# A decoder layer in which gated linear attention runs beside the branch projections and its inputs are computed in pairs

## The chip, the cores and the metric

The kernel runs on one core of a Trainium2 chip. TensorE multiplies matrices (PE in the profile; PEld are its weight loads, which overlap the products), VectorE (DVE) does elementwise arithmetic, ScalarE (ACT) activations, copies and biases, GpSimd (POOL) fills and a few transfers, and SyncE (SP) issues most of the transfers. The metric is device time of one execution in microseconds, lower is better; a kernel's time is the median of several executions.

## What is computed

One layer of a decoder for 512 prompt positions and 8 x 8 sample positions, 576 columns in all, model width 2048, float32. One projection of the input feeds three token mixers: S5 (a diagonal state space model), GLA (gated linear attention, 4 heads) and a convolution over 31 taps. Each mixer's output is multiplied by its gate path, projected to the model width, scaled by a sigmoid merge gate and summed; the sum goes through w_o.

```python
proj = x @ w_in + b_in
(s5_u, s5_z, q, k, v, a_low, gla_z, ca, cb, cz, gates) = jnp.split(proj, _split_points(), axis=-1)
y_s5, s5_re_new, s5_im_new = s5_mixer(s5_u, ...)
y_s5 = jax.nn.gelu(y_s5)
y_s5 = y_s5 * jax.nn.sigmoid(y_s5 @ w_glu + b_glu)
br_s5 = (y_s5 * jax.nn.silu(s5_z)) @ p_s5
o_gla, gla_new = gla_mixer(q, k, v, a_low, gla_s, gla_w_a2, gla_b_a, gla_norm_g)
br_gla = (o_gla * jax.nn.silu(gla_z)) @ p_gla
y_c, conv_new = conv_mixer(ca, cb, conv_buf, conv_w, conv_b, conv_ln_g, conv_ln_b)
br_conv = (y_c * jax.nn.silu(cz)) @ p_conv
g_s5, g_gla, g_conv = jnp.split(jax.nn.sigmoid(gates), N_BRANCH, axis=-1)
out = (g_s5 * br_s5 + g_gla * br_gla + g_conv * br_conv) @ w_o
h = DN_ALPHA * x + out
h = h + jax.nn.sigmoid(h @ w_pg) * (p @ w_pe)
return layer_norm(h, ln_g, ln_b), ...
```

Inside conv_mixer, g = ca * sigmoid(cb) is convolved per channel with 31 taps, then normalised over the channels.

## The kernel before, in words

**Precision and products.** A float32 operand is split into a high part in the type fp32r (`hi`, an ACT copy) and the rest (`lo`, a DVE subtraction). A product of two operands is three matmuls: hi by hi, hi by lo, lo by hi. Columns are held as two halves of 288, so that a matmul has the form 128x288 with a contraction of 128.

**Jobs.** The big products are a list of jobs of three kinds, which `run_jobs` works off in order. A *single* makes one tile of 128 output rows. With 16 contraction tiles it is 96 matmuls (line 433); with 8, in w_glu and the three branch projections p_gla, p_s5 and p_conv, it is 48 ("short"). A *pair* makes two tiles of 128 rows at once by seven half sized products in the manner of Strassen and Winograd (`PRODUCTS`, line 462): 7 x 24 = 168 matmuls where two singles need 192. It needs sums of the weights (DVE, `raw<-raw` and `raw<-raw,sl`) and sums of the input, the forms S1 to S4, which `make_forms` prepares once for w_in and `m_forms` once more for w_o. After some of the seven products ACT or DVE copies or adds a partial result out of PSUM: "a" after the first (from `mm`) and the second (from `aux`). A *quad* (line 543) is a small product for w_pe.

**Background work.** Everything else (S5's scan, GLA's decay and heads, the convolution, its norm, the splitting of the mixers' outputs) is written as generators that are advanced by `pump` between pieces of the jobs: BG_RATE 1.1 in full singles, BG_SHORT 0.5 in short ones, BG_PAIR 0.2 in pairs, each times the length of the piece; a generator's `yield` names the cost of the step it has done. Groups in SLOW are a lane of their own. `need(key)` drives the background until a result is there. A scheduler then orders the instructions of each engine; tiles come from 71 slots of 128x576 floats in SBUF, and a generator waits when too few are free.

**The order of the work.** First 8 jobs for s5_u with the S5 blocks beside them, 6 gate tiles as singles, the job `a` (the decay's low rank input), then the 16 tiles k, q and v of the four heads as singles, head after head (`plain` keeps them in SBUF), with a GLA head spawned after each head's tiles; after that 4 more gate tiles as singles and `make_forms`. Then the pairs: 8 for the convolution's inputs ca and cb, 12 for s5_z, gla_z and cz, 19 for the other 38 gate tiles; the convolution tiles run beside them. A convolution tile is, per tap, one DVE operation on 512 prompt columns and one on the 64 sample columns (line 98). Then w_glu (8 short jobs), p_gla, p_s5 and p_conv (16 each), whose results are multiplied by their gates and summed in SBUF in `self.A` by `br_job`; beside p_conv `m_forms` makes the forms of the sum for w_o, a quad follows, then w_o in 8 pairs, another quad, w_pg and the layer norm.

Of the kernel before, what the change touches and what calls it, by code (L numbers as in the profile page):

```python
# [30 lines left out]
BG_RATE, BG_SHORT, BG_PAIR = 1.1, 0.5, 0.2  # L31
WIDTH = dict(s5=3)
SLOW = ("forms", "conv", "conv_norm")
# [5 lines left out]
NFILL = (0, 0, 0, 4, 6)  # L39
# [4 lines left out]
class K:  # L44
# [274 lines left out]
    def run_jobs(self):  # L319
# [201 lines left out]
        for u in range(first, nu):  # L521
            ji, k0, n = units[u]
            if self.jobs[ji][0] == "pair" or self.jobs[ji][1].shape[0] < D:
                self.reserve = 0
            while npr < nu and (npr <= u + 1 or at[npr] - at[u] < PREP):
                prep(npr)
                npr += 1
            load_to(u)
            if n is None:
                run_pair(u)  # L530
                continue
            kind, w, col, xs, evac, before, after, dual = self.jobs[ji]
            if kind == "quad":
                if before is not None:
                    before()
                xh, xl = xs()
                hv = halves.pop(u)
                for j in range(4):
                    ps = self.ps_mm.tile([128, 1024], F32, name="mm")
                    for k, (_, _, hi, lo) in enumerate(hv):  # L540
                        for lh, rh, a, b in ((hi, xh, k == 0, False), (hi, xl, False, False), (lo, xh, False, k == 1)):
                            for o, c, m in FULL:
                                nc.tensor.matmul(ps[:, o:o + m], lh[:, j], rh[k][:, c:c + m], start=a, stop=b)  # L543
                    evac(j, ps)
                    self.pump(BG_SHORT * 1.6)
                continue
            nk = w.shape[0] // 128
            if k0 == 0:
                if before is not None:
                    before()  # L550
                pss[ji] = self.ps_mm.tile([128, 1024], F32, name="mm")
            xs = xs() if callable(xs) else xs
            hv = halves.pop(u)
            rate = BG_RATE if nk == KT else BG_SHORT
            for z, (ka, m, hi, lo) in enumerate(hv):
                for c in range(0, m, 2):
                    mms(pss[ji], (ka + c, 2, hi[:, c:], lo if lo is None else lo[:, c:]), xs, nk,
                        PARTS[:1] if dual in (1, 2) else FULL)
                    if z < len(hv) - 1 or c < m - 2:
                        self.pump(rate * 1.6)  # L560
            if dual in (1, 2):
                kept.append((ji, xs, hv))
            if k0 + n == nk:
                if dual in (1, 2):
                    evac(pss[ji], 0)
                else:
                    evac(pss.pop(ji))
                if after is not None:
                    after()
            self.pump(rate * 1.6)  # L570
# [28 lines left out]
    def make_forms(self):  # L599
# [529 lines left out]
    def gla_decay(self):  # L1129

        nc = self.nc
        self.mk = self.alloc()
# [5 lines left out]
        nc.gpsimd.memset(wa, 0.0)  # L1138
        for r in (0, 16):
# [81 lines left out]

    def gla_head(self, h):
        nc = self.nc
        q, k, cum = self.q[h], self.k[h], self.cum[h]
# [3 lines left out]
        for s in range(2):  # L1228
            vc = self.v[2 * h + s]
# [138 lines left out]
        self.done.add(f"head{h}")  # L1368
        if h == 3:
            self.free(*self.gt, self.gm)  # L1370
        mv, rs = self.gmv[:, h], self.grs[:, h]
# [56 lines left out]

    def conv_tile(self, n):
# [110 lines left out]
    def br_job(self, name, br, n, y, key=None, extra=None, last=None, order=range(16)):  # L1540
        w = self.i[name][0]

        def load(m):
            if m is not None:
                self.gate[m] = self.alloc()
                self.nc.sync.dma_start(self.gate[m], self.gd[br, m])

        def before():
            if n == order[0]:
                self.gate = {}  # L1550
                load(n)
                self.need(key)
# [16 lines left out]
    def build(self):
# [11 lines left out]
        self.kd = self.dram.tile([8, 128, 256], F32, name="kd")  # L1581
        self.jobs = []
        w_in = self.i["w_in"][0]
        X = (self.xh, self.xl)
        self.q, self.k, self.v, self.u = [None] * 4, [None] * 4, [None] * 8, [None] * 8
        self.A = [None] * 16

        def evac_a(ps):
# [3 lines left out]
            self.alow = t  # L1592
            self.spawn(self.gla_decay(), "gla_decay")
# [56 lines left out]
        fill(NFILL[4])  # L1650
        self.job(w_in, OFF["a"], X, evac_a, lambda: [x_out(k) for k in range(8)], dual=3)
        for h in range(4):
            for nm, st in (("k", self.k), ("q", self.q)):
                self.job(w_in, OFF[nm] + h * 128, X, self.plain(st, h, OFF[nm] + h * 128),
                         (lambda h=h: self.need(f"head{h - 2}")) if h > 1 and nm == "k" else None)
            for s in range(2):
                c = OFF["v"] + (2 * h + s) * 128
                self.job(w_in, c, X, self.plain(self.v, 2 * h + s, c),
                         after=(lambda h=h: self.spawn(self.gla_head(h), "gla")) if s else None)
            if h == 1:  # L1660
                self.jobs[-1] = self.jobs[-1][:5] + (lambda: [x_out(k) for k in range(8, 16)],) + self.jobs[-1][6:]
            if h == 2:
                self.jobs[-1] = self.jobs[-1][:6] + (lambda: (self.spawn(self.gla_head(2), "gla"),
                                                            self.spawn(self.make_forms(), "forms")),) + self.jobs[-1][7:]
            fill(NFILL[h])

# [47 lines left out]
        def y_make(br, out):  # L1714
            while br == 2 and "conv" not in self.done:
# [16 lines left out]
        def w_free(p):  # L1732
# [78 lines left out]
        for n in range(8):  # L1811
# [12 lines left out]
            self.job(self.i["w_glu"][0], n * 128, parts(ys), evac, lambda n=n: glu_before(n))  # L1824
        self.done.add("y0")
# [414 lines left out]
```

## Time and profile before

| what | value |
|---|---|
| median of 3 runs | 2334.5 us (2333.52 to 2338.45) |
| the profiled execution, its own time | 2337.35 us |
| its span in the profile | 2335.5 us |
| PE busy | 2271.5 us, 97% |
| DVE busy | 1748.7 us, 75% |
| ACT busy | 1003.7 us, 43% |
| POOL busy | 55.2 us, 2% |
| moved by DMA | 324.67 MB, mean 139 GB/s |

The page gives the busy time of each engine, the busy share of 40 slices of the span, the chain that ended last and the costliest groups of instructions. The trace also answers by stretches of time: busy time of each engine, the clock granted to TensorE (PEclk, 1.00 is full speed) and the share of the DMA engines. The stages in the trace, from the first PE instruction of each: s5_u from 7.6 us, six gates to 261.8, `a` to 281.7, k, q, v to 557.8, four gates to 622, the convolution's pairs to 807, the pairs of s5_z, gla_z and cz to 1090, the gate pairs to 1526, w_glu to 1591, p_gla to 1697, p_s5 to 1801, p_conv to 1903, w_o from 1910 to 2090 and w_pg to 2327.

### The profile page before, as it was taken

To read this page: it belongs to the slowest core of one execution; us is meant where nothing else is said; L and a number is where in the kernel's file an instruction comes from. 1 tells how busy PE (TensorE), PEld (TensorE's weight loads), DVE (VectorE), ACT (ScalarE), POOL (GpSimd) and SP (SyncE) were. 2 spreads that over 40 slices of the span, in tenths; PEclk is the share of its full clock that TensorE was granted. 3 is DMA by queue.
4 is the path that set the end of the run, shared out by engine and by line. 5 is a ranking of instruction groups with operands and counts; after the bars stand their busy time and mean duration, and the time that the engine had idled before them with its cause. 6 is when DMAs were issued, how large, how long until landed. Compare 5 with 4: busy or idle time off the path is not lost.

```text
span 2335.5 us, 44279 instructions
## 1 busy us (share of the span) xinstructions
PE 2271.5 (97%) x17084; PEld 2227.2 (95%) x17084; DVE 1748.7 (75%) x3449; ACT 1003.7 (43%) x1970; POOL 55.2 (2%) x105
## 2 busy tenths in 40 slices
PE   8899999999999999999999999999999999999998
PEld 7889899999999999999999999999999999999997
DVE  4687665555889798898979888799576777784556
ACT  4344437434454544444554554552232344452221
POOL 1100000000000000000000000000000000000000
PEclk9999999999999999999999999999999999999998
DMA  8955543343434444434443444476566344464322
GB/s 232 239 127 114 125 103 85 106 122 106 141 100 124 124 121 126 119 118 133 121 138 112 145 122 121 153 254 224 167 193 199 115 127 148 155 194 141 102 83 82
DMA packets 426131, 324.67 MB, mean 139 GB/s; under 512 B 49630, under 2 KB 374938, under 8 KB 425904
## 3 DMA queue, kind: packets, MB, share of 16 engines
q1 hardware_dynamic: 420768, 309.69, 45.0%
q0 software_dynamic: 5152, 12.16, 2.1%
q8 instruction: 134, 2.20, 0.4%
q14 instruction: 77, 0.63, 0.1%
HBM read 254.01 MB, written 68.44 MB: 138 GB/s over the span
## 4 chain that ended last, share of the span: by engine, by line
PE 53%; DVE 1%; DMA 1%; ACT 0%; issue 0%; SPq 0%; DVEq 0%; ACTq 0%
PE mm L433 23%; PE mm L462 16%; PE aux L462 12%; PE mm L543 1%; DVE sl L80 1%; DVE sl L98 1%; PE two L102 0%; DMA sl<-zd 0%; ACT hi L73 0%; DMA sl<-gd 0%; DMA pd<-sl 0%; DVE lo L80 0%; ACT sl L73 0%; DMA gd<-sl 0%; PE mm L2036 0%
## 5 line engine op out<-in xcount | busy, mean ns | idle before, releaser
L433 PE MATMUL mm<-sl,hi 128*128 128x288 f32 (+1 forms) x5024 | 909.8, 301 | 11.5 <-ACT sl L73 7.1
L73 ACT ACTIVATE hi<-raw 128x512 fp32r<-128x512 f32 x784 | 490.7, 630 | 771.6 <-PE mm L433 390.7
L433 PEld LDWEIGHTS mm<-sl,hi 128*128 128x128 f32 x5024 | 751.1, 191 | 19.6 <-ACT sl L73 7.8
L80 DVE TENSOR_TENSOR lo<-raw,hi 128x512 fp32r<-128x512 f32 x780 | 534.5, 686 | 292.8 <-ACT hi L73 283.5
L462 PE MATMUL mm<-sl,hi 128*128 128x288 f32 x3008 | 609.2, 297 | 8.8 <-ACT sl L73 4.7
L433 PE MATMUL mm<-sl,lo 128*128 128x288 f32 (+1 forms) x2480 | 542.9, 298 | 0.0
L462 PEld LDWEIGHTS mm<-sl,hi 128*128 128x128 f32 x3008 | 485.1, 189 | 10.7 <-ACT sl L73 5.4
L462 PE MATMUL aux<-sl,hi 128*128 128x288 f32 x2256 | 451.4, 295 | 5.5 <-ACT hi L73 4.6
L80 DVE TENSOR_TENSOR sl<-sl,sl 128x576 f32<-128x576 f32 (+9 forms) x696 | 382.7, 582 | 87.4 <-ACT sl L73 40.9
L462 PE MATMUL mm<-sl,lo 128*128 128x288 f32 x1504 | 443.5, 297 | 1.5 <-DVE lo L80 1.5
L433 PEld LDWEIGHTS mm<-sl,lo 128*128 128x128 f32 x2480 | 404.1, 190 | 2.5 <-issue 1.6
L462 PEld LDWEIGHTS aux<-sl,hi 128*128 128x128 f32 x2256 | 360.3, 188 | 7.5 <-ACT hi L73 6.3
L462 PE MATMUL aux<-sl,lo 128*128 128x288 f32 x1128 | 332.4, 295 | 0.2 <-DVE lo L80 0.2
L462 PEld LDWEIGHTS mm<-sl,lo 128*128 128x128 f32 x1504 | 284.0, 189 | 1.9 <-DVE lo L80 1.9
L98 DVE SCALAR_TENSOR_TENSOR sl<-sl,cw,sl 128x512 f32<-128x512 f32 (+1 forms) x480 | 235.6, 511 | 0.3
L462 PEld LDWEIGHTS aux<-sl,lo 128*128 128x128 f32 x1128 | 211.9, 188 | 0.8 <-DVE lo L80 0.7
L80 DVE TENSOR_TENSOR raw<-raw,sl 128x512 f32<-128x512 f32 x282 | 190.0, 683 | 9.2 <-DMA sl<-in_w_in 5.5
L73 ACT ACTIVATE sl<-sl 128x576 fp32r<-128x576 f32 (+11 forms) x291 | 127.7, 463 | 117.0 <-DVE sl L80 72.3
L80 DVE TENSOR_TENSOR lo<-sl,hi 128x512 fp32r<-128x512 f32 x196 | 132.7, 686 | 46.1 <-ACT hi L73 44.8
L73 ACT ACTIVATE hi<-sl 128x512 fp32r<-128x512 f32 x196 | 120.9, 628 | 97.4 <-PE mm L462 66.0
L73 ACT ACTIVATE sl<-aux 128x288 f32<-128x288 f32 (+9 forms) x197 | 66.6, 353 | 71.1 <-PE aux L102 25.9
L73 ACT ACTIVATE sl<-mm 128x288 f32<-128x288 f32 (+3 forms) x130 | 59.4, 457 | 54.0 <-PE mm L462 17.7
(183 smaller groups left out, 1116.9 us busy)
## 6 DMA issues: line engine op xcount, KB each, us to landing
raw<-in_w_in SPq DMA_DIRECT2D x144, 512.0 KB
sl<-in_w_in SPq DMA_DIRECT2D x164, 256.0 KB
raw<-in_w_pg SPq DMA_DIRECT2D x32, 512.0 KB
gd<-sl SPq DMA_DIRECT2D x48, 288.0 KB
sl<-gd SPq DMA_DIRECT2D x48, 288.0 KB
raw<-in_p_gla SPq DMA_DIRECT2D x16, 512.0 KB
raw<-in_p_s SPq DMA_DIRECT2D x16, 512.0 KB
raw<-in_p_conv SPq DMA_DIRECT2D x16, 512.0 KB
```

What stands on the lines that cost most here:

```text
L73: return self.nc.scalar.activation(out, in_, func, **kw)
L80: self.nc.vector.tensor_tensor(out, a, b, op)
L98: self.nc.vector.scalar_tensor_tensor(out, a, s, b, op0=op0, op1=op1)
L433: nc.tensor.matmul(ps[:, o:o + n], lh[:, k - ka], rh[k][:, c:c + n], start=a, stop=b)
L462: nc.tensor.matmul(ps[bank], lh[:, k - ka], rh[k], start=bool(a), stop=b, skip_group_check=not opens)
L543: nc.tensor.matmul(ps[:, o:o + m], lh[:, j], rh[k][:, c:c + m], start=a, stop=b)
```

## The change

- **q, k and v in pairs.** The 16 single jobs become 8 pairs behind the convolution's pairs. Their evacuation adds the bias and stores to DRAM (`qd`); a head loads its four tiles again (`gla_load`). The result of `a` goes to DRAM too (`ad`). 12 gate tiles are singles where 10 were, and 18 gate pairs remain of 19. `make_forms` is spawned by the job `a`.
- **GLA beside the branches.** The decay and the four heads are spawned in the last gate pair, and so run beside w_glu, p_s5 and p_conv. The order of the branches is p_s5, p_conv, a quad, p_gla.
- **The sum in DRAM.** p_s5 stores its gated result (`sd`), p_conv adds to it by an accumulating transfer on POOL's queue, p_gla loads it, adds its own share and makes the forms for w_o, for which there is no quad between p_gla and w_o any more.
- **The convolution's samples.** The 30 operations on 64 columns a tile become four groups of two products (128 x 248: 8 positions by 31 taps, an overlapping view of the samples against the weights) and one reduction over the taps, and an ACT operation for the bias.
- **Rates.** BG_PAIR is 0.27, the short jobs have rates by name, and "yc" is in the slow lane.

```diff
-BG_RATE, BG_SHORT, BG_PAIR = 1.1, 0.5, 0.2
+BG_RATE, BG_SHORT, BG_PAIR = 1.1, 0.5, 0.27
+RATES = dict(w_glu=0.4, p_s5=1.0, p_conv=1.0, p_gla=0.3)
 WIDTH = dict(s5=3)
-SLOW = ("forms", "conv", "conv_norm")
+SLOW = ("forms", "conv", "conv_norm", "yc")
...
-NFILL = (0, 0, 0, 4, 6)
+NFILL = 12
...
-            rate = BG_RATE if nk == KT else BG_SHORT
+            rate = BG_RATE if nk == KT else self.rates.get(id(self.jobs[ji]), BG_SHORT)
...
-            while len(self.free_slots) < (10 if "gla" in self.done else 22):
+            while len(self.free_slots) < (10 if "s5" in self.done else 24):
...
     def gla_decay(self):
...
+        while len(self.free_slots) < 22:
+            yield None
...
+        self.alow = self.alloc()
+        nc.sync.dma_start(self.alow, self.ad)
...
+    def gla_load(self, h):
+
+        t = [self.alloc() for _ in range(4)]
+        for x, n in zip(t, (h, 4 + h, 8 + 2 * h, 9 + 2 * h)):
+            self.nc.sync.dma_start(x, self.qd[n])
+        self.kqv[h] = t
+
     def gla_head(self, h):
         nc = self.nc
-        q, k, cum = self.q[h], self.k[h], self.cum[h]
+        while len(self.free_slots) < 18:
+            yield None
+        if h not in self.kqv:
+            self.gla_load(h)
+            yield
+            yield
+        k, q, *vv = self.kqv.pop(h)
+        cum = self.cum[h]
...
+    @staticmethod
+    def taps(x):
+
+        return bass.AP(tensor=x.tensor, offset=x.offset, ap=[x.ap[0], [1, 8], [1, 31]])
...
-        ys = y[:, 512:].rearrange("p (s e) -> p s e", s=8)
         w = self.cw[:, n]
         self.ts(y[:, :512], g[:, 0:512], w[:, 0:1], self.vc("conv_b", n))
-        self.ts(ys, gs[:, :, 0:8], w[:, 0:1], self.vc("conv_b", n))
         for k in range(1, 31):
             self.stt(y[:, :512], g[:, k:k + 512], w[:, k:k + 1], y[:, :512])
-            self.stt(ys, gs[:, :, k:k + 8], w[:, k:k + 1], ys)
-            yield 0.85
+            yield 0.75
+
+        ys = y[:, 512:].rearrange("p (s e) -> p s e", s=8)
+        pr = g[:, :496].rearrange("p (s e k) -> p s e k", s=2, e=8)
+        for s in range(0, 8, 2):
+            for z in range(2):
+                self.mul(pr[:, z], self.taps(gs[:, s + z]), w[:, None, :].to_broadcast([128, 8, 31]))
+            nc.vector.tensor_reduce(ys[:, s:s + 2], pr, axis=mybir.AxisListType.X, op=OP.add)
+            yield 1.4
+        self.act(y[:, 512:], y[:, 512:], AF.Identity, bias=self.vc("conv_b", n))
...
             g = self.gate.pop(n)
             self.mul(self.s2(g), self.v2(ps), self.s2(g))
-            if br == 1:
-                self.A[n] = g
+            if mode == "first":
+                self.nc.sync.dma_start(self.sd[n], g)
+            elif mode == "more":
+                self.nc.gpsimd.dma_start(self.sd[n], g, accum_op=OP.add)
             else:
                 self.add(self.A[n], self.A[n], g)
-                self.free(g)
+            self.free(g)
         self.job(w, n * 128, lambda: ([a for a, _ in y], [b for _, b in y]), evac, before)
+        self.rates[id(self.jobs[-1])] = RATES[name]
...
-            self.alow = t
-            self.spawn(self.gla_decay(), "gla_decay")
+            nc.sync.dma_start(self.ad, t)
+            self.free(t)
+            self.spawn(self.make_forms(), "forms")
...
-        for h in range(4):
-            for nm, st in (("k", self.k), ("q", self.q)):
...
-            fill(NFILL[h])
+        fill(NFILL)
+        self.jobs[-1] = self.jobs[-1][:5] + (lambda: [x_out(k) for k in range(8, 16)],) + self.jobs[-1][6:]
...
+                self.spawn(self.gla_decay(), "gla_decay")
+                for h in range(4):
+                    self.spawn(self.gla_head(h), "gla")
                 self.spawn(y_make(1, yg), "yg")
+                self.spawn(y_make(2, yc), "yc")
+
+        def kqv_pair(n, col):
+            def evac(t0, X0, t1):
+                b0, b1 = self.bcol(col), self.bcol(col + 128)
+                self.act(t0[:, H:], X0, AF.Identity, bias=b0)
+                self.act(t0[:, :H], t0[:, :H], AF.Identity, bias=b0)
+                self.act(t1, t1, AF.Identity, bias=b1)
+                for z, t in enumerate((t0, t1)):
+                    nc.sync.dma_start(self.qd[n + z], t)
+                self.free(t0, t1)
+            return col, evac
...
+        for nm, n0, w in (("k", 0, 4), ("q", 4, 4), ("v", 8, 8)):
+            pairs += [kqv_pair(n0 + n, OFF[nm] + n * 128) for n in range(0, w, 2)]
...
-            self.br_job("p_gla", 1, n, yg, "y1", (lambda: drop(ys)) if n == 0 else None)
+            self.br_job("p_s5", 0, n, yz, "y0", "first")
         for n in range(16):
-            self.br_job("p_s5", 0, n, yz, "y0", (lambda: (drop(yg), self.spawn(y_make(2, yc), "yc"))) if n == 0 else None)
+            self.br_job("p_conv", 2, n, yc, "y2", "more", (lambda: drop(yz)) if n == 0 else None)
+        pe_quad(2)
...
-            self.br_job("p_conv", 2, n, yc, "y2", lambda i=i: c_extra(i), order=order)
-        pe_quad(2)
+            self.br_job("p_gla", 1, n, yg, "y1", "last", lambda i=i: c_extra(i), order=order)
```

How the instructions of an engine stand in both kernels, at three places. Rows with the same form one behind the other are one row with a count.

ACT in the third pair of s5_z, gla_z and cz, before. `hi<-raw` prepares weights for a later product; `sl_10240` and `sl_10202` are the tiles that the pair before leaves; `sl_10291` is tile "a" of this pair, copied out of the first product (`mm`) and the second (`aux`).

```order
L73 ACTIVATE hi<-raw 128x512
L73 ACTIVATE sl_10240<-sl_10202,bias 128x288
L73 ACTIVATE hi<-raw 128x512
L73 ACTIVATE sl_10240<-mm,bias 128x288
L73 ACTIVATE sl_10291<-mm 128x288
L73 ACTIVATE sl_10291<-aux 128x288
L73 ACTIVATE hi<-raw 128x512 x2
L73 ACTIVATE hi<-sl_10136 128x512
```

The same place now; `sl_9811` is tile "a" there.

```order
L74 ACTIVATE hi<-raw 128x512
L74 ACTIVATE sl_9752<-sl_9713,bias 128x288
L74 ACTIVATE sl_9752<-mm,bias 128x288
L74 ACTIVATE hi<-raw 128x512
L74 ACTIVATE sl_9811<-mm 128x288
L74 ACTIVATE hi<-raw 128x512
L74 ACTIVATE hi<-sl_9648 128x512
L74 ACTIVATE hi<-sl_9650 128x512
L74 ACTIVATE hi<-raw 128x512 x2
L74 ACTIVATE sl_9811<-aux 128x288
L74 ACTIVATE hi<-sl_9782 128x512
```

The copy out of the second product stood ahead of the next preparations; now five preparations of weights stand ahead of it, between the two copies.

PE with a GLA head beside a single job of k, q, v, before (line 433 the job, lines 1276 to 1300 and 102 the head).

```order
L433 MATMUL mm<-sl_86,lo 128x288
L1300 MATMUL two<-sl_4764,sl_4723 128x256
L1299 MATMUL aux<-sl_4764,sl_4723 128x256
L1276 MATMUL aux<-sl_3945,sl_4874 128x64
L1277 MATMUL aux<-sl_4874,sl_4872 128x64
L102 MATMUL aux<-ident,sl_3758 128x128
L433 MATMUL mm<-sl_86,lo 128x288
```

The same operations of a head now, beside a short job of a branch (line 434 the job, lines 1295 to 1319 and 103 the head).

```order
L434 MATMUL mm<-sl_17921,lo 128x288
L1319 MATMUL two<-sl_18915,sl_18839 128x256
L434 MATMUL mm<-sl_17921,lo 128x288
L1318 MATMUL aux<-sl_18915,sl_18839 128x256
L1295 MATMUL aux<-sl_18881,sl_19011 128x64
L1296 MATMUL aux<-sl_19011,sl_19009 128x64
L103 MATMUL aux<-ident,sl_18880 128x128
L434 MATMUL mm<-sl_17992,hi 128x288 x2
```

The head's operations stand among the matmuls of a branch projection in the same small groups as they stood among those of k, q and v.

PE from the last short job of the branches into w_o, before (line 433 the job, line 543 the quad, line 462 w_o; `sl_21623` and the like are the form S1, one tile for each of 8 contraction steps).

```order
L433 MATMUL mm<-sl_21320,lo 128x288 x2
L543 MATMUL mm<-sl_17374,hi 128x288 x2
L543 MATMUL mm<-sl_17375,hi 128x288 x2
L543 MATMUL mm<-sl_17374,lo 128x288 x2
L543 MATMUL mm<-sl_17617,hi 128x288 x2
L543 MATMUL mm<-sl_17618,hi 128x288 x2
L543 MATMUL mm<-sl_17617,lo 128x288 x2
L462 MATMUL aux<-sl_21623,hi 128x288
```

The start of w_o now: `sl_22531`, `sl_22824` and `sl_22845` are the form A11 at the contraction steps 5, 6 and 7, `sl_21785` to `sl_22834` S1 at the steps 0 to 6.

```order
L463 MATMUL mm<-sl_22531,hi 128x288 x2
L463 MATMUL mm<-sl_22531,lo 128x288
L463 MATMUL aux<-sl_21785,hi 128x288
L463 MATMUL aux<-sl_21786,hi 128x288
...
L463 MATMUL aux<-sl_22834,hi 128x288
L463 MATMUL aux<-sl_22833,lo 128x288
L463 MATMUL mm<-sl_22824,hi 128x288 x2
L463 MATMUL mm<-sl_22824,lo 128x288
L463 MATMUL mm<-sl_22845,hi 128x288 x2
```

Quad matmuls stood between the last job and w_o; now 21 matmuls of the second product S1 stand between the steps 5 and 6 of the first.

More of the change, by code (lines that the diff above doesn't have):

```diff
@@ L1228, in gla_head @@
         for s in range(2):
-            vc = self.v[2 * h + s]
+            vc = vv[s]
             self.stack(self.vpad, vc[:, 512:], 1, 2)
@@ L1367, in gla_head @@
         self.free(q, k, kd, kq, vs, *vt)
-        self.done.add(f"head{h}")
         if h == 3:
             self.free(*self.gt, self.gm)
+        elif len(self.free_slots) > 10:
+            self.gla_load(h + 1)
         mv, rs = self.gmv[:, h], self.grs[:, h]
@@ L1538, in plain, with br_job @@
         return evac
-    def br_job(self, name, br, n, y, key=None, extra=None, last=None, order=range(16)):
+    def br_job(self, name, br, n, y, key, mode, extra=None, order=range(16)):
         w = self.i[name][0]
@@ L1546, in load @@
                 self.nc.sync.dma_start(self.gate[m], self.gd[br, m])
+                if mode == "last":
+                    self.A[m] = self.alloc()
+                    self.nc.sync.dma_start(self.A[m], self.sd[m])
         def before():
@@ L1550, in before @@
                 self.gate = {}
+                self.need(key)
                 load(n)
-                self.need(key)
             load(dict(zip(order, order[1:])).get(n))
@@ L1581, in build @@
         self.kd = self.dram.tile([8, 128, 256], F32, name="kd")
+        self.ad = self.dram.tile([128, T], F32, name="ad")
+        self.qd = self.dram.tile([16, 128, T], F32, name="qd")
+        self.sd = self.dram.tile([16, 128, T], F32, name="sd")
+        self.kqv, self.rates = {}, {}
         self.jobs = []
@@ L1584, in build @@
         X = (self.xh, self.xl)
-        self.q, self.k, self.v, self.u = [None] * 4, [None] * 4, [None] * 8, [None] * 8
+        self.u = [None] * 8
         self.A = [None] * 16
@@ L1648, in build @@
             self.job(w_in, c, X, lambda ps, n=n: self.s5_store_u(n, ps))
-        fill(NFILL[4])
         self.job(w_in, OFF["a"], X, evac_a, lambda: [x_out(k) for k in range(8)], dual=3)
-        for h in range(4):
-            for nm, st in (("k", self.k), ("q", self.q)):
[L1654 to L1664, printed above, removed]
-            fill(NFILL[h])
+        fill(NFILL)
+        self.jobs[-1] = self.jobs[-1][:5] + (lambda: [x_out(k) for k in range(8, 16)],) + self.jobs[-1][6:]
         ys, yg, yz, yc, G, P = ([None] * 8, [None] * 8, [None] * 8, [None] * 8, [None] * 8, [])
@@ L1714, in y_make @@
         def y_make(br, out):
-            while br == 2 and "conv" not in self.done:
+            while br == 2 and not {"conv", "y0"} <= self.done:
                 yield None
@@ L1823, in evac @@
                 self.free(t)
-            self.job(self.i["w_glu"][0], n * 128, parts(ys), evac, lambda n=n: glu_before(n))
-        self.done.add("y0")
+            self.job(self.i["w_glu"][0], n * 128, parts(ys), evac, lambda n=n: glu_before(n),
+                     (lambda: (drop(ys), self.done.add("y0"))) if n == 7 else None)
+            self.rates[id(self.jobs[-1])] = RATES["w_glu"]
         for n in range(16):
-            self.br_job("p_gla", 1, n, yg, "y1", (lambda: drop(ys)) if n == 0 else None)
+            self.br_job("p_s5", 0, n, yz, "y0", "first")
         for n in range(16):
-            self.br_job("p_s5", 0, n, yz, "y0", (lambda: (drop(yg), self.spawn(y_make(2, yc), "yc"))) if n == 0 else None)
+            self.br_job("p_conv", 2, n, yc, "y2", "more", (lambda: drop(yz)) if n == 0 else None)
+        pe_quad(2)
         MF = {f: ([None] * UK, [None] * UK) for f in ("S1", "S2", "S3", "S4", "A11", "A12", "A22")}
@@ L1849, in c_extra @@
             if i == 0:
-                drop(yz)
+                drop(yc)
             elif i % 2 == 0 and i < 14:
@@ L1863, in o_before @@
             if n == 0:
-                drop(yc)
+                drop(yg)
                 for k in (6, 7):
```

2 lines of the change are left out of this document (removed).

## The prediction

> **What bounds the kernel now.** First the page: span, busy times, and DVE's busy tenths in 40 slices.
>
> ```profile
> span 2335.5 us, 44279 instructions
> PE 2271.5 (97%) x17084; PEld 2227.2 (95%) x17084; DVE 1748.7 (75%) x3449; ACT 1003.7 (43%) x1970; POOL 55.2 (2%) x105
> DVE  4687665555889798898979888799576777784556
> ```
>
> PE is busy for 97% of the span, so matmuls taken away shorten it, unless DVE, at 8 and 9 tenths wherever pairs run, becomes the later one. Then the chain that ended last, a product of a pair and a run of short jobs (start, length, what):
>
> ```profile
> 1035.87 3.20 PE mm L462 x24
> 1781.70 121.82 PE mm L433 x912
> ```
>
> Both give 0.1333 us a matmul (3.20 / 24, 121.82 / 912) with nothing between. So a pair of 168 is 22.4 us, a single of 96 is 12.8, a short job of 48 is 6.4. Then the stages (length, busy time of PE, PEld, DVE, ACT and POOL, PEclk, DMA share, GB/s): k, q, v in two halves; the convolution's pairs; the pairs of s5_z, gla_z and cz ("z"); the gate pairs; w_glu; p_gla; p_s5; p_conv.
>
> ```profile
> 282.00:420.00 138.00, 134.63 (x1050) 130.89 (x1049) 80.67 (x168) 70.33 (x146) 5.93 (x14) 0.98 0.36 92
> 420.00:558.00 138.00, 138.00 (x1062) 129.49 (x1061) 81.25 (x221) 55.88 (x133) 10.22 (x15) 1.00 0.41 122
> 622.00:807.00 185.00, 182.57 (x1366) 182.04 (x1365) 153.92 (x282) 93.79 (x173) 6.39 (x18) 0.99 0.41 117
> 807.00:1090.00 283.00, 272.87 (x2027) 270.07 (x2026) 250.32 (x463) 134.79 (x247) 2.21 (x4) 0.99 0.42 123
> 1090.00:1526.00 436.00, 429.53 (x3209) 428.19 (x3209) 379.17 (x692) 223.48 (x408) 4.44 (x8) 0.99 0.45 134
> 1526.00:1591.00 65.00, 64.23 (x482) 63.99 (x482) 64.31 (x116) 31.26 (x52) 0.00 (x0) 1.00 0.71 230
> 1591.00:1697.00 106.00, 104.10 (x776) 103.37 (x776) 73.60 (x131) 29.69 (x50) 1.12 (x2) 1.00 0.63 206
> 1697.00:1801.00 104.00, 103.51 (x774) 103.09 (x773) 76.25 (x118) 31.72 (x50) 0.00 (x0) 1.00 0.65 201
> 1801.00:1910.00 109.00, 109.00 (x819) 109.00 (x819) 79.33 (x133) 39.20 (x65) 0.00 (x0) 1.00 0.35 105
> ```
>
> A z pair takes 283 / 12 = 23.58 us, a gate pair 436 / 19 = 22.95: 1.18 and 0.55 above 22.4. The z stage alone leaves PE idle for 10.1 us. Its waits (total, times, longest), and one of them in time:
>
> ```profile
> PE aux L462 <- ACT hi L73: 4.6, 6, 1.3
> PE mm L462 <- ACT hi L73: 4.1, 4, 1.0
> PE mm L462 <- DVE lo L80: 1.5, 1, 1.5
> ```
>
> ```profile
> 859.61 0.29 PE L462 MATMUL aux<-sl,lo 128*128 128x288 f32 x1
> 859.94 0.41 ACT L73 ACTIVATE sl<-aux 128x288 f32<-128x288 f32 x1 [2.75 <-PE aux L462]
> 860.24 1.14 ACT L73 ACTIVATE hi<-raw 128x512 fp32r<-128x512 f32 x2
> 860.92 0.53 PE L462 MATMUL mm<-sl,hi 128*128 128x288 f32 x2 [1.02 <-ACT hi L73]
> ```
>
> ACT stands idle for 2.75 us until PE has ended a product, because the copy `sl<-aux` is next on it; the `hi` behind it is what PE's next product needs, and PE waits. That is an order of ACT, not a lack of time: ACT is busy for 134.79 of 283 us. The clock suffers too:
>
> ```profile
> 883.00:887.00 4.00, 2.47 (x17) 2.01 (x16) 2.57 (x5) 2.75 (x6) 0.00 (x0) 1.00 0.35 101
> 887.00:891.00 4.00, 4.00 (x21) 4.00 (x20) 4.00 (x9) 1.41 (x3) 0.00 (x0) 0.57 0.18 40
> 891.00:895.00 4.00, 4.00 (x32) 4.00 (x32) 3.81 (x9) 2.15 (x4) 0.00 (x0) 1.00 0.39 100
> ```
>
> After 1.5 us of idle time, 21 matmuls fit where 32 do at full clock: 11 x 0.1333 = 1.5 us more.
>
> **The change, part by part.**
>
> *Matmuls.* Sixteen singles become 8 pairs: 8 x 168 - 16 x 96 = -192. Two more gate singles for one gate pair: +24. Together -168, all on PE's path, -168 x 0.1333 = **-22.4 us**.
>
> *What pairs cost beyond matmuls.* Seven more pairs. At the gate pair's 0.55: **+3.9**; between 0 and the z pair's 1.18 (+8.3). Their evacuation is three ACT operations and two stores like a gate pair's, therefore the gate pair's row.
>
> *The z waits.* In the new order the copy out of the second product has five preparations of weights ahead of it, so the wait at 859.94 holds nothing back. I take a z pair down to a gate pair: 283 - 12 x 22.95 = **-7.6**; between 0 (the waits come back elsewhere) and -14.2 (down to 22.4).
>
> By the Trainium skill, "TensorE: Matmul & The Clock Gate", section on HAM oscillation, only PE-idle gaps longer than about 3.4 us bring the clock down. The rows at 883 to 891 show otherwise, with 1.5 us; by that rule the 1.5 us would not belong to the waits, and the z term would be -6.1.
>
> *The start of p_gla.* It waits twice for the splits of GLA's output:
>
> ```profile
> 1604.06 0.53 PE L433 MATMUL mm<-sl,hi 128*128 128x288 f32 x2 [1.10 <-DVE sl L80]
> 1606.18 0.79 PE L433 MATMUL mm<-sl,hi 128*128 128x288 f32 x4 [0.80 <-DVE sl L80]
> ```
>
> Now p_gla is last, and its splits can be made beside p_conv. The first branch is p_s5, which wants the last tile of w_glu only 42 matmuls, 5.6 us, after its start: **-1.9**; at worst 0, if p_s5 or p_conv waits as long.
>
> *GLA beside the branches.* Its PE work moves and is neither more nor less. In k, q, v it took with S5's rest 276 - 16 x 12.8 = 71 us of PE, and PE was idle there for 3.4 us in all, one wait:
>
> ```profile
> PE aux L102 <- ACT sl L73: 3.4, 1, 3.4
> ```
>
> What hides its chains is DVE's spare time. The four branch stages have 293.5 us of DVE in 384. GLA brings at most 161.9 (k, q, v) less the singles' own weight preparation; per single four `lo` (row below), 16 x 2.74 = 44: 118. So 411 in 384 + 71 = 455 us, 90%, no more than a pair stage. Its order on PE is as before, small groups among matmuls. **0**; between -3.4 (that wait goes) and +13.6 (one such wait a head).
>
> *Stores, loads, the sum in DRAM.* They are 4 x 4 loads of a head, 16 stores of qd, 16 stores, 16 accumulations and 16 loads of sd, 288 KB each: 80 x 0.295 = 24 MB on 325. w_glu took 0.71 of the DMA engines at 230 GB/s with PE busy for 64.23 of 65, so the branches can carry more. The stores sit on SP's queue behind the DVE or ACT operation that fills them, with weight loads queued behind; `zd` and `gd` stores stand so in the pairs now. The nearest price of an accumulation (last column: us to landing):
>
> ```profile
> xd<-sl POOLq DMA_DIRECT2D x16, 288.0 KB, 13.0
> ```
>
> p_gla's second tile (8) is accumulated by p_conv's ninth job, 7 jobs or 45 us before p_gla begins: 13 is covered by 32. On POOL behind it stand only GLA's fills. **0**; without that cover +13 once.
>
> *The samples of the convolution.* The DVE rows (busy, mean ns):
>
> ```profile
> L80 DVE TENSOR_TENSOR lo<-raw,hi 128x512 fp32r<-128x512 f32 x780 | 534.5, 686 | 292.8 <-ACT hi L73 283.5 <-PE two L102 2.9 <-DMA sl<-in_w_in 0.9
> L98 DVE SCALAR_TENSOR_TENSOR sl<-sl,cw,sl 128x512 f32<-128x512 f32 x240 | 178.5, 745 | 0.0
> L98 DVE SCALAR_TENSOR_TENSOR sl<-sl,cw,sl 128x64 f32<-128x64 f32 x240 | 66.7, 278 | 0.2
> L80 DVE TENSOR_TENSOR sl<-sl,sl 128x256 f32<-128x256 f32 x90 | 35.7, 424 | 1.8 <-ACT sl L73 1.3
> L1964 DVE BATCH_NORM_STATS2 ystat<-sl 128x6 f32<-128x512 f32 x12 | 8.2, 683 | 0.1
> ```
>
> Before, 30 x 0.278 = 8.3 us a tile. Now four groups of two products (nearest, 128x256: 0.424) and a reduction over 496 (nearest, the statistics over 512: 0.683): 4 x 1.53 = 6.1. Off PE's path: **0**, unless a group is far dearer (rival C).
>
> *BG_PAIR.* A pair gave the background 7 x 3.2 x 0.2 = 4.5 named us, now 6.0. A tap is named 0.85 and takes 1.02 before, 0.75 and 0.745 now: 5.4 us of DVE a pair before, 6.0 now. A z pair, at 250.32 / 12 = 20.9 us of DVE, becomes 21.5 of 22.4. Still under, by little: **0**; its bad case is rival A.
>
> *Seams.* From the singles into the pairs the forms must be ready: the convolution stage, this seam in it, lost 2.4 us of PE in all, so 0 to +2.4. At w_o the quad is gone as cover, but 21 matmuls of S1, 2.8 us, stand before A11's sixth step, against a product, a sum, a copy and a difference of the last job, four operations of 0.4 to 0.75: 0 to +3. **0** for both.
>
> Sum: -22.4 + 3.9 - 7.6 - 1.9 = **-28.0 us**. The profiled execution took 2337.35 us itself (2335.5 of span), 2.85 above the median of 2334.5. 2337.35 - 28.0 = 2309.35, less 2.85: **2306.5 us**.
>
> **Rivals.**
>
> *A: the waits stay.* DVE in z pairs is at 21.5 of 22.4, and any pair may get its ACT or DVE operations in a poor order. For it: ten waits on ACT in this stage at half load of ACT. Against: the new order. The z term is gone and the new pairs cost 1.18: -22.4 + 8.3 - 1.9 = -16, **2318.5**.
>
> *B: GLA holds the branches.* A head is a chain PE, ACT, DVE, PE, and short jobs leave 6.4 us a tile. One wait of 3.4 a head: -28 + 13.6, **2320**. Against: 0 us of idle PE in 420 to 558 beside the same heads.
>
> *C: slower, by the reduction.* No row shows a reduction, nor an operand that overlaps itself. If a group costs much more than 1.53, the pairs become bound by DVE. Its spare time where the taps run is 31.1 (convolution) + 32.7 (z) + 56.8 (gates) = 120.6 us. It decides against the change when 32 groups cost more than 120.6 + 28 beyond 1.53 each, from 6.2 us a group. At 7 us: 32 x 5.5 - 120.6 - 28 = +27, **2361.5**. Against: 9 times the statistics' time for the same elements. The Trainium skill, "VectorE: DVE Perf Modes", rules for kernel authors, calls tensor_reduce the slowest DVE operation and advises restructuring; it speaks against this edit, and no run here shows one.
>
> **How the numbers follow.** Forecast 0.64, A 0.19, B 0.09, C 0.05; 0.03 for a gain beyond 35. The low end adds the GLA wait (-3.4) and frees the new pairs of their 3.9 and the z pairs of part of theirs: -39, **2295**. The high end takes in A and B with a little over: **2322**. Outside lie C, part of B and the large gain. About 0.2% (4.7 us) is what a measurement of this kernel can tell from no change. Faster by over that (below 2329.8): forecast, A, most of B and the large gain, **0.91**; within it 0.04 (B with two waits a head); slower 0.05 (C).
>
> **What would show it.** 168 fewer matmuls of line 434 and 463 at the same 0.1333 us. The z pairs near 22.95 us, with ACT's waits gone; if the pairs stand near 23.6, A. PE idle in p_s5 and p_conv under 4 us, or else B. A reduction near 0.7 us and a product near 0.42; several us would be C. Accumulations landing well before p_gla loads. A time outside 2295 to 2322 makes the prediction wrong, and so does the right time with the z waits still there.

## The result, and the profile after

The changed kernel takes 2298.03 us (median of 4 runs, 2295.69 to 2300.79) beside 2335.98 us before (median of 4 runs; the 2334.5 above is the median of three): ratio 0.9838, 95% interval 0.982 to 0.9856. It is faster by 38 us, where 28 were forecast; 2298.0 lies inside the range, 8.5 us below the forecast of 2306.5. Of the two profiled executions the one before is high among its runs (2337.35) and the one after the lowest of its own (2295.69), so that their spans differ by 41.6 us.

The page after, span and busy times:

```profile
span 2293.9 us, 44353 instructions
PE 2236.8 (98%) x16916; PEld 2194.7 (96%) x16916; DVE 1786.0 (78%) x3400; ACT 1036.2 (45%) x2048; POOL 69.7 (3%) x121
```

There are 168 matmuls fewer, 16916 for 17084, and PE is busy for 98%. The stages after (length, busy PE, PEld, DVE, ACT, POOL, PEclk, DMA share, GB/s): the convolution's pairs, the new pairs of q, k, v, the pairs of s5_z, gla_z and cz ("z"), the gate pairs, p_s5, p_conv, p_gla.

```profile
377.00:560.00 183.00, 179.85 (x1360) 179.53 (x1359) 155.44 (x265) 92.79 (x175) 6.40 (x18) 1.00 0.40 116
560.00:741.00 181.00, 179.44 (x1354) 179.18 (x1353) 165.82 (x284) 90.69 (x168) 1.09 (x2) 1.00 0.45 135
741.00:1009.00 268.00, 268.00 (x2025) 267.94 (x2024) 247.26 (x425) 134.42 (x247) 2.22 (x4) 1.00 0.43 125
1009.00:1416.00 407.00, 405.69 (x3049) 404.24 (x3049) 362.10 (x611) 216.55 (x396) 3.91 (x7) 1.00 0.48 146
...
1484.00:1623.00 139.00, 133.39 (x1002) 126.10 (x1001) 87.22 (x207) 69.47 (x149) 8.02 (x12) 1.00 0.64 197
1623.00:1760.00 137.00, 132.12 (x1001) 125.40 (x1001) 76.44 (x183) 44.77 (x103) 20.17 (x25) 1.00 0.83 234
1766.00:1868.00 102.00, 102.00 (x767) 102.00 (x766) 73.85 (x124) 36.60 (x61) 0.00 (x0) 1.00 0.47 143
```

The row to look at is the third: PE is busy for 268.00 of 268 us, 22.3 us a pair, with ACT and DVE as busy as before. The z stage does not wait any more. The gate pairs take 407 / 18 = 22.6 us each, the new pairs 181 / 8 = 22.6. The spans differ like this:

| part | forecast, us | spans, us | how the second number comes |
|---|---|---|---|
| 168 matmuls | -22.4 | -22.4 | 168 x 0.1333, counted, not measured apart |
| z pairs | -7.6 | -15 | 283 to 268 |
| gate pairs, beyond their matmuls | 0 | -6.6 | 436 - 19 x 22.4 = 10.4 to 407 - 18 x 22.4 = 3.8 |
| new pairs, beyond theirs | +3.9 | +1.8 | 181 - 8 x 22.4 |
| p_gla | -1.9 | -4 | 106 to 102, of which 1.9 are its two waits |
| the rest, GLA's new place in it | 0 | +4.6 | what is left of -41.6 |

What the gate pairs lost before were two single waits (PE's waits from 1090 to 1526 us before; total, times, longest). The longer one is not even a pair's: line 543 is the first of two quads that stand between the last gate pair and w_glu in both kernels.

```profile
PE mm L543 <- DVE lo L80: 4.3, 1, 4.3
PE mm L462 <- ACT sl L73: 2.0, 1, 2.0
```

After (1009 to 1416 us) one is left, again a quad's:

```profile
PE mm L544 <- DVE lo L81: 1.3, 1, 1.3
```

What took the other waits of this stage away stays open.

ACT in the third z pair after, which answers to the rows of before at 859 us:

```profile
789.92 0.63 ACT L74 ACTIVATE hi<-raw 128x512 fp32r<-128x512 f32 x1 [0.35 <-DVE raw L81]
790.46 1.14 ACT L74 ACTIVATE hi<-sl 128x512 fp32r<-128x512 f32 x2
791.50 1.38 ACT L74 ACTIVATE hi<-raw 128x512 fp32r<-128x512 f32 x2
792.78 0.40 ACT L74 ACTIVATE sl<-aux 128x288 f32<-128x288 f32 x1
```

Five preparations of weights start while PE works on the second product, and the copy `sl<-aux` comes when that product is done, without an idle time of ACT ahead of it. PE is less well off in p_s5 and p_conv, where GLA's heads now run. Its waits from 1484 to 1760 us:

```profile
PE aux L1318 <- ACT sl L74: 5.7, 4, 2.2
PE aux L103 <- ACT sl L74: 2.0, 1, 2.0
PE two L103 <- ACT sl L74: 1.5, 1, 1.5
PE two L1319 <- ACT sl L74: 0.9, 1, 0.9
PE aux L1374 <- DVE sl L99: 0.5, 1, 0.5
```

They are 10.6 us, all in front of background operations, the heads' above all, where beside k, q and v it was one wait of 3.4. The 7 us more are in the last row of the table.

Last the operations of which no row was to be had before (line, operation, count, busy time, mean ns), and the accumulation's us to landing:

```profile
L81 DVE TENSOR_TENSOR sl<-sl,cw 128x248 f32<-128x248 f32 x64 | 23.5, 407 | 0.0
L1488 DVE TENSOR_REDUCE sl<-sl 128x16 f32<-128x496 f32 x32 | 21.1, 658 | 0.0
```

```profile
sd<-sl POOLq DMA_DIRECT2D x16, 288.0 KB, 5.8
```

A group of two products and a reduction takes 2 x 0.407 + 0.658 = 1.47 us; 1.53 were estimated.

### The profile page after: what moved, and what is told of

It is laid out like the page before. It is cut to its first block, busy times and chain, and to the rows that moved or that the text cites. A ratio compares the mean times of both kernels' runs of the same rounds, so it can differ in the third digit from the quotient of the medians.

```text
span 2293.9 us, 44353 instructions
## 1 busy us (share of the span) xinstructions
PE 2236.8 (98%) x16916; PEld 2194.7 (96%) x16916; DVE 1786.0 (78%) x3400; ACT 1036.2 (45%) x2048; POOL 69.7 (3%) x121
## 4 chain that ended last, share of the span: by engine, by line
PE 82%; issue 7%; DMA 4%; DVE 3%; SPq 2%; ACT 1%; POOL 0%; DVEq 0%; POOLq 0%; ACTq 0%
PE mm L463 30%; PE mm L434 27%; PE aux L463 22%; DVE sl L81 2%; PE mm L544 1%; SPq L960 1%; DMA raw<-in_w_in 1%; PE aux L103 1%; PE two L103 1%; ACT sl L74 1%; DMA sl<-yd 0%; DMA gx<-sl 0%; DVE lo L81 0%; DMA sd<-sl 0%; PE two L1033 0%
## 5 line engine op out<-in xcount | busy, mean ns | idle before, releaser
L434 PE MATMUL mm<-sl,hi 128*128 128x288 f32 (+1 forms) x4128 | 748.3, 300 | 7.8 <-ACT sl L74 5.7
L463 PE MATMUL mm<-sl,hi 128*128 128x288 f32 x3456 | 695.7, 295 | 6.4 <-ACT sl L74 5.6
L434 PEld LDWEIGHTS mm<-sl,hi 128*128 128x128 f32 x4128 | 615.7, 190 | 14.9 <-ACT sl L74 6.7
L463 PEld LDWEIGHTS mm<-sl,hi 128*128 128x128 f32 x3456 | 553.2, 188 | 7.9 <-ACT sl L74 6.3
L463 PE MATMUL aux<-sl,hi 128*128 128x288 f32 x2592 | 518.5, 294 | 0.3 <-ACT hi L74 0.3
L463 PE MATMUL mm<-sl,lo 128*128 128x288 f32 x1728 | 507.7, 295 | 0.0
L434 PE MATMUL mm<-sl,lo 128*128 128x288 f32 (+2 forms) x2032 | 448.8, 299 | 0.0
L81 DVE TENSOR_TENSOR sl<-sl,sl 128x576 f32<-128x576 f32 (+12 forms) x680 | 368.5, 577 | 97.5 <-ACT sl L74 46.0
L463 PEld LDWEIGHTS aux<-sl,hi 128*128 128x128 f32 x2592 | 414.3, 188 | 0.7 <-ACT hi L74 0.6
L463 PE MATMUL aux<-sl,lo 128*128 128x288 f32 x1296 | 381.3, 294 | 0.0
L99 DVE SCALAR_TENSOR_TENSOR sl<-sl,cw,sl 128x512 f32<-128x512 f32 x240 | 178.4, 743 | 0.2
```

The source lines that it names most:

```text
L81: self.nc.vector.tensor_tensor(out, a, b, op)
L99: self.nc.vector.scalar_tensor_tensor(out, a, s, b, op0=op0, op1=op1)
L434: nc.tensor.matmul(ps[:, o:o + n], lh[:, k - ka], rh[k][:, c:c + n], start=a, stop=b)
L463: nc.tensor.matmul(ps[bank], lh[:, k - ka], rh[k], start=bool(a), stop=b, skip_group_check=not opens)
```

## The experiments

Theory T says that the z waits went because of the edit of the convolution's samples; R1 that the higher BG_PAIR did it; R2 that the pairs' new place did. Later theories: L, that a convolution not done by the end of the pairs makes the branches wait, against G (GLA waits there anyway) and D (the higher rate fills DVE); and H, that the rate of the short jobs does not set GLA's cost.

### The samples as before, in the changed kernel

```diff
+            self.stt(ys, gs[:, :, k:k + 8], w[:, k:k + 1], ys)
+            yield 0.85
-            yield 0.75
...
-            nc.vector.tensor_reduce(ys[:, s:s + 2], pr, axis=mybir.AxisListType.X, op=OP.add)
```

> The changed kernel with the convolution's samples as before (30 operations on 64 columns a tile and the old named cost of 0.85), everything else of the change kept. Theory T: the waits of PE on ACT in the pairs of s5_z, gla_z and cz went because this edit lightened the DVE work beside the pairs, which let the scheduler put the weight preparations ahead of the copies. Then the waits come back here: those pairs take 23.2 to 23.8 us each instead of 22.3, and the time is 2306 to 2314 us. Rival R1 (the higher BG_PAIR made the order better) and rival R2 (the place of the pairs behind the eight new ones did): the pairs stay at 22.3 and the time at 2298 +- 3 us.

2319.46 us (ratio to before 0.9938, 0.9926 to 0.9951). The z stage and its waits:

```profile
746.00:1024.00 278.00, 270.06 (x2023) 267.87 (x2022) 262.50 (x498) 133.22 (x245) 3.34 (x6) 1.00 0.40 120
```

```profile
PE aux L463 <- ACT hi L74: 4.1, 5, 1.3
PE mm L463 <- ACT hi L74: 3.1, 3, 1.0
```

```profile
820.97 0.41 ACT L74 ACTIVATE sl<-aux 128x288 f32<-128x288 f32 x1 [2.75 <-PE aux L463]
821.28 1.14 ACT L74 ACTIVATE hi<-raw 128x512 fp32r<-128x512 f32 x2
```

The same wait as before the change, with ACT idle for the same 2.75 us ahead of the copy. T holds, R1 and R2 fall for this. The time is 5 us above what T allowed: beside the 10 us of the z stage the other stages of this profile are some 11 us longer than in the changed kernel's, none by more than 3 if p_s5 and p_conv are taken together (275 us for 276). Why they are stays open.

### The samples alone, in the kernel before

> The kernel before with only the new convolution samples (two products and one reduction for every two samples, named costs 0.75 and 1.4). T: the pairs of s5_z, gla_z and cz go from 23.6 to about 22.4 us, and the whole from 2336 to 2322 us (2319 to 2327). R1 and R2: the waits stay, 2336 +- 3 us.

The edit is the one above the other way round. 2324.39 us, ratio 0.9965 (0.9952 to 0.9977). The z stage and p_conv:

```profile
808.00:1076.00 268.00, 268.00 (x2025) 267.93 (x2024) 246.82 (x425) 135.99 (x251) 2.21 (x4) 1.00 0.45 133
...
1779.00:1893.00 114.00, 106.56 (x778) 105.52 (x777) 80.93 (x136) 39.39 (x65) 0.00 (x0) 0.96 0.41 126
```

The z stage is that of the changed kernel, with PE busy throughout, so the samples are enough for it. But p_conv now takes 113 us instead of 102, with two waits:

```profile
PE mm L433 <- ACT sl L73: 7.4, 2, 5.0
```

What it waits for is its operand y_c. A convolution tile is now named 30 x 0.75 + 4 x 1.4 = 28.1 us where it was 30 x 0.85 = 25.5, so a pair's credit buys less of it: the last tap starts 63 us into p_gla, 50 us before.

### The samples and BG_PAIR 0.27, in the kernel before

```diff
-BG_RATE, BG_SHORT, BG_PAIR = 1.1, 0.5, 0.2
+BG_RATE, BG_SHORT, BG_PAIR = 1.1, 0.5, 0.27
```

> The kernel before with the new convolution samples and BG_PAIR 0.27, nothing else of the change. Theory L (a convolution that is not done by the end of the pairs is what makes the branches wait): the taps end in the gate pairs, some 300 us earlier than alone, p_conv's waits of about 10 us in the run with the samples alone go, and the time is 2312 us (2308 to 2317). Rival D (the higher rate fills DVE in the pairs): the pairs get waits and nothing is won on the 2324 of the samples alone.

2316.1 us, ratio 0.9933 (0.992 to 0.9945). z and p_conv:

```profile
808.00:1077.00 269.00, 267.89 (x2023) 267.58 (x2022) 257.14 (x442) 135.56 (x249) 2.21 (x4) 1.00 0.45 130
...
1781.00:1883.00 102.00, 102.00 (x767) 102.00 (x766) 72.91 (x121) 35.97 (x60) 0.00 (x0) 1.00 0.35 107
```

p_conv's waits are gone, as L said, though the taps do not end in the gate pairs: the last one starts at 1560 us. DVE is busy for 96% of the z stage, where it was 94% with the waits in the run with the old samples, and PE is idle for 1.1 us only: the waits go with the order on ACT, not with DVE's load. By the ratios, of the change's 1.62% these two edits alone give 0.67%; the remaining 0.95% are 22 us, by the medians as they stand 18. The intervals leave some 5 us either way, so this agrees with the 22.4 that 168 matmuls are worth and does not measure them.

### BG_PAIR 0.2, in the changed kernel

> The changed kernel with BG_PAIR 0.2 instead of 0.27. T and R2: no wait in the pairs of s5_z, gla_z and cz; 2298 +- 4 us, unless the background that is put off is missing at the branches. R1: the waits return, those pairs take over 23 us and the time is 2306 us or more.

2330.18 us, ratio 0.999 (0.998 to 1.0): without this one number the whole gain is lost. The z stage stays at 268 us, so R1 falls here too. Lost is the stretch where p_s5 passes into p_conv:

```profile
1616.00:1690.00 74.00, 51.82 (x273) 41.40 (x272) 53.40 (x148) 41.70 (x93) 5.55 (x8) 0.70 0.74 242
```

```profile
PE aux L1296 <- ACT sl L74: 4.7, 1, 4.7
PE aux L1295 <- ACT sl L74: 3.7, 1, 3.7
PE aux L1318 <- ACT sl L74: 3.0, 3, 1.5
```

In 74 us PE has 273 matmuls, waits for the heads' operations and runs at a clock of 0.70. The rows of the taps from 1416 us on:

```profile
L99 DVE SCALAR_TENSOR_TENSOR sl<-sl,cw,sl x30: 727/745/752, 1438.8 to 1493.6; 128x512 f32<-128x512 f32 x30
```

In the changed kernel the last tap starts at 1272.6 us. The code says what follows: the first job of p_conv calls `need("y2")`, which steps the background until y_c is there, and it steps the lane of the heads first. Between the first matmul of p_conv and the start of its third job the trace has 153 matmuls of the background, in the changed kernel 26. That the heads stand there because of `need` is read from the code; no run takes them out of the lane.

### q, k and v as singles, in the changed kernel

```diff
-            pairs += [kqv_pair(n0 + n, OFF[nm] + n * 128) for n in range(0, w, 2)]
...
+                self.job(w_in, OFF[nm] + n * 128, X, evac)
```

> The changed kernel with q, k and v as 16 single jobs that store to DRAM, in place of the 8 pairs; GLA still runs beside the branches. 192 matmuls more at 0.1333 us are +25.6, less the 1.5 us that the eight pairs lost beyond their matmuls: 2322 us (2318 to 2326) if matmuls are what the pairs saved. Rival: the singles would be hidden by or would relieve the DVE, and cost less than 15 us: below 2313.

2347.16 us, ratio 1.0062 (1.005 to 1.0075), 25 us more than expected and slower than before the change. 38 pairs instead of 46 at the same rate give the convolution less; p_conv:

```profile
1649.00:1812.00 163.00, 143.18 (x1010) 132.60 (x1009) 90.80 (x225) 54.92 (x122) 22.06 (x28) 0.92 0.77 220
```

Here the last tap starts at 1498 us and 137 matmuls of the background stand in p_conv's first two jobs. To tell whether that is the cause:

### The same with BG_PAIR 0.33

> The changed kernel with q, k and v as single jobs, as in the run that took 2347, and BG_PAIR 0.33 in place of 0.27, so that 38 pairs give the convolution as much as 46 did. L: its taps end before the last gate pair, p_s5 and p_conv go from 295 to about 276 us, and the time is 2298 + 25 = 2323 us (2318 to 2328). Rival G (GLA beside the branches waits anyway, since without the eight pairs something else is late): 2340 or more. Rival D: the pairs pass 22.6 us on average and the time stays above 2330.

2322.3 us, ratio 0.9961 (0.9947 to 0.9974), as L expected. p_s5 and p_conv:

```profile
1512.00:1653.00 141.00, 137.09 (x1027) 129.44 (x1027) 95.42 (x228) 75.20 (x165) 7.67 (x12) 1.00 0.70 220
1653.00:1786.00 133.00, 130.24 (x976) 123.56 (x975) 72.93 (x176) 40.51 (x90) 20.27 (x25) 0.99 0.82 227
```

The taps end at 1370 us, 34 matmuls of the background stand in p_conv's first two jobs, and both stages take 274 us together, where the changed kernel has 276. L holds, G and D fall. The time is 24 us above the changed kernel by the medians, 29 by the ratios; the price of 192 matmuls, 25.6, less what the new pairs lose lies at the lower end of that.

### The samples four times over

```diff
+            for _ in range(4):
                 for z in range(2):
                     self.mul(pr[:, z], self.taps(gs[:, s + z]), w[:, None, :].to_broadcast([128, 8, 31]))
                 nc.vector.tensor_reduce(ys[:, s:s + 2], pr, axis=mybir.AxisListType.X, op=OP.add)
```

> The changed kernel with each group of the convolution's samples computed four times over (the same output): 32 x 3 x 1.47 = 141 us more of DVE, a group costing 5.9 us. By the arithmetic of rival C, in which the spare DVE time of the pairs is used up first (27.6 + 15.2 + 20.7 + 44.9 = 108 us in the changed kernel): 2298 + 33 = 2331 us (2321 to 2341). By L on top of it, the convolution is late and the branches wait as well: 2345 to 2370. If spare DVE time cannot be used, since every delay of a weight preparation holds PE: 2298 + 141 = 2439.

2375.93 us, ratio 1.0191 (1.0177 to 1.0205). Pairs of z and gates, then p_conv:

```profile
762.00:1052.00 290.00, 273.79 (x2022) 271.83 (x2021) 281.81 (x515) 132.89 (x249) 3.33 (x6) 0.97 0.40 116
1052.00:1498.00 446.00, 412.56 (x3051) 408.81 (x3050) 416.59 (x742) 216.62 (x396) 2.80 (x5) 0.97 0.44 134
...
1703.00:1839.00 136.00, 131.07 (x995) 124.46 (x995) 76.18 (x182) 44.38 (x102) 20.18 (x25) 1.00 0.82 234
```

That is above both ranges given for spare DVE time that is used up first. All 78 us fall in the pairs; the branches are unchanged. So rival C's mechanism, a dear group that holds PE up in the pairs, is real, and its price was too low: of 141 us of added DVE work 141 - 78 = 63 cost nothing, where 108 were counted on. PE loses the time in a few long waits, 66 us in 16 of them. The longest rows (380 to 1498 us):

```profile
PE mm L463 <- ACT sl L74: 34.2, 4, 17.5
PE aux L463 <- ACT hi L74: 16.2, 4, 11.8
PE mm L463 <- ACT hi L74: 11.0, 2, 10.7
```

The added work comes bunched, 17.6 us at the end of each of eight tiles, so that a sum of spare time over a whole stage may be the wrong measure; no run spreads it out. On a straight line between the two kernels, a rough estimate, the gain would be gone from about 1.47 + 4.4 x 38 / 78 = 3.6 us a group, not from 6.2.

### Rates, sum and quad

All in the changed kernel. First the rate 0.5 for all short jobs (`RATES = dict(w_glu=0.5, p_s5=0.5, p_conv=0.5, p_gla=0.5)`):

> The changed kernel with the rate 0.5 in all short jobs, as before the change, in place of rates by name. On PE the last operation of the heads then stands at the start of p_gla instead of two thirds into p_conv. Theory H: what GLA costs beside the branches is its own PE work and waits of a few us that do not depend on the rate, but p_gla then waits for GLA's output, up to 10 us: 2300 to 2310 us. Rival: the rate sets the waits; with the heads stretched out the branches lose their 24 us beyond PE's own work, and the time is below 2292.

2310.9 us, ratio 0.9913 (0.9897 to 0.9929), 1 us above the range of H. p_s5 and p_conv together take 275 us, so the waits do not thin out; the heads end late, the quad takes 12 us and p_gla 107. H holds against its rival here. Then the sum on DVE, for which p_conv also loads the stored share:

```diff
-                self.nc.gpsimd.dma_start(self.sd[n], g, accum_op=OP.add)
+                self.add(g, self.A[n], g)
+                self.free(self.A[n])
+                self.nc.sync.dma_start(self.sd[n], g)
```

> The changed kernel, but p_conv loads the stored share, adds on DVE and stores the sum through SP, in place of the accumulating transfer of POOL's queue. 16 additions of 0.75 us are 12 us of DVE and 16 loads of 288 KB more, in a stage where DVE is busy for 76 of 137 us: 2298 us (2295 to 2302) if the accumulation is hidden in the changed kernel and DVE has room. Rival: the accumulations of the changed kernel hold something back, then 2294 or less; or DVE's additions come before GLA's chains, then 2303 or more.

2293.63 us, ratio 0.984 (0.9826 to 0.9853), where the rival that the accumulations hold something back was put (2294 or less); and with the rates of p_s5 and p_conv at 0.6:

> The changed kernel with the sum added on DVE in p_conv and the rates of p_s5 and p_conv at 0.6 instead of 1.0, so that the heads end 11 short jobs... that is, within the last quarter of p_conv, still ahead of p_gla. H: 2291 to 2298 us, like the run with the sum on DVE (2293.6). Rival (the rate sets the waits): below 2290.

2289.38 us, ratio 0.9817 (0.9803 to 0.983), below H's range and by 0.6 us where its rival was put; with the quad behind p_gla again instead (`pe_quad(2)` moved):

> The changed kernel with the sum added on DVE in p_conv and the quad put back between p_gla and w_o. The two waits of 1.2 us at the start of w_o in the changed kernel go if the quad covers them; GLA's output is wanted 6.4 us earlier, which its end in p_conv allows: 1 to 2 us less than the run with the sum on DVE, 2292 us (2288 to 2296). Rival: no difference, since before the change w_o started with one wait of 1.2 us behind the quad as well.

2291.45 us, ratio 0.9823 (0.9808 to 0.9837), as expected; and the changed kernel beside them:

> The changed kernel itself once more, on the same chip as the runs with the sum on DVE. If the accumulation on POOL's queue costs nothing it stands within 2 us of them; if it costs what the profiles show in p_conv (136.1 us against 131.7), 4 to 5 us above.

2296.82 us, ratio 0.9845 (0.9827 to 0.9862). The three versions have medians 3 to 7 us below the changed kernel, with intervals that overlap with its own. Taken together their 14 runs have a mean of 2291.9 us, the changed kernel's 8 runs (the first 4 were made at another time) 2297.2; 5.3 us is nearly four standard errors. Beside the 4 runs made with them alone it is 4.4 us and two. So the sum on DVE is probably faster by some 5 us; which of the three versions is the best is not shown. The profiles agree: p_conv takes 131 us with the sum on DVE,

```profile
1623.00:1754.00 131.00, 129.99 (x990) 123.80 (x989) 85.06 (x197) 44.14 (x102) 6.81 (x10) 1.00 0.83 274
```

and 136 in both profiles of the changed kernel. By which path the accumulation costs these 5 us stays open. At the rate 0.6 it is 134 and 137 us for p_s5 and p_conv, 271 in all as with 1.0. That speaks for H, but it is the profile of the slowest of five runs (2295.13 us), and the median speaks for the rival, so for rates between 0.5 and 1.0 H is not settled.

## Why the prediction was right, and where it was wrong

**The matmuls** were right as far as the runs can tell: -22.4 us. The run with singles and a full convolution stands 24 to 29 us above the changed kernel, for 25.6, and the two small edits alone leave 18 to 22 us to be explained by the rest of the change.

**The z pairs.** "I take a z pair down to a gate pair" failed: -7.6 was forecast, -15 came, just beyond the other end of the range given there (-14.2). The mechanism, an order on ACT, was right. Wrong was the yardstick. The gate pair's 0.55 us was an average with two waits and their slower clock in it; a z pair without waits costs nothing beyond its matmuls, 22.3 us. The same error made the new pairs too dear (+3.9 for +1.8) and missed the gate pairs' own -6.6. These misses all make the gain larger. That the time still came within 8.5 us of the forecast is in part luck, since GLA's place took 7 us back that the sum did not have.

**The samples and BG_PAIR.** Both stood at 0 "off PE's path". In work that was right: 1.47 us a group for 1.53. The Trainium skill, "VectorE: DVE Perf Modes", rules for kernel authors, warns of tensor_reduce as the slowest DVE operation; here 496 elements took 0.658 us, less than the statistics over 512 (0.683), and the edit replaced 31 operations a tile (the first tap and 30 more) with 12 and one of ACT. But the two edits do more than their own time. The samples' edit is the one that changed the order on ACT, in either kernel, and BG_PAIR decides whether GLA fits beside the branches. Pricing each edit by its busy time found neither. Which part of the samples' edit does it, the operations that are gone or the smaller named cost, is not shown: no run has one without the other.

**GLA beside the branches** was forecast at 0. p_s5 and p_conv take 276 us, 71 more than their 32 x 6.4; k, q and v took 71 more than their matmuls before. The two 71 are equal by chance: the earlier one had S5's rest in it and 3.4 us of idle PE, the later one has 10.5. By the sign that the prediction named, idle PE under 4 us in p_s5 and p_conv or else B, rival B came true in part: 7 us more than before in eight short waits, half of the 13.6 that it priced, and inside the bounds of this term (-3.4 to +13.6). Its time of 2320 did not come. And it can be far worse: with BG_PAIR 0.2 p_s5 and p_conv take 310 us instead of 276. One wait a head was B's price; what happens there is a burst of the heads at once, because `need` finds y_c unfinished. That place, a `need` with the heads ahead in the lane, was in the code, and no term of the sum stands for it.

**Rival A** did not occur. **Rival C** did not either, and its arithmetic took all spare DVE time of the pairs as usable, of which 63 of 108 us were in the run with the fourfold groups. **p_gla, stores and loads, the start of w_o** came as said: p_gla starts without a wait, an accumulation lands in 5.8 us for a bound of 13.0, and w_o starts with waits of 0.9, 0.9 and 0.3 us where 0.9, 0.3 and 0.2 stood before. But landing in time is not being free: the sum on DVE is probably some 5 us faster.

## What to carry to other kernels

Before a stage's excess is taken for the price of its work, look for the single waits in it; what remains may be nothing. An edit that costs an engine no time can still change the order in which a scheduler puts the work, and so be the larger part of a result: test each small edit alone and in both kernels. And where background work is forced by a due date, ask what stands ahead of it in the lane, since all of that will be driven too.

## What the runs showed of the hardware

The clock after an idle stretch of PE is not settled by the length of the stretch alone. In the changed kernel PE waits at the same place in the convolution's pairs in two profiles. First the profile above: PE's first row after the wait, with the length of the wait in brackets, and the next 4 us.

```profile
476.74 0.53 PE L463 MATMUL mm<-sl,hi 128*128 128x288 f32 x2 [3.15 <-ACT sl L74]
477.00:481.00 4.00, 4.00 (x32) 4.00 (x32) 2.79 (x5) 1.52 (x3) 0.00 (x0) 1.00 0.10 31
```

Then the same kernel's second profile:

```profile
474.76 0.53 PE L463 MATMUL mm<-sl,hi 128*128 128x288 f32 x2 [3.34 <-ACT sl L74]
476.00:480.00 4.00, 4.00 (x21) 4.00 (x20) 2.19 (x4) 1.16 (x2) 0.00 (x0) 0.57 0.00 0
```

After 3.15 us of idle time the clock stayed, with 32 matmuls in 4 us; after 3.34 us it averaged 0.57 in the 4 us that begin 1.2 us later, with 21. These two alone would allow a limit between them, but before the change 1.5 us, in two waits of 1.0 and 0.5, had been enough at 883 us. So a wait of a few us costs its own length and, at some moments, 1.5 us more; that may be part of the spread of some 5 us among runs of one kernel.
